# Doubling a block-triangular inverse: paired array corners and evictions on two engines

## The chip, the cores and the metric

The kernel runs on one core of a Trainium2 chip. The core has TensorE (PE in the views; PEld is its weight load), VectorE (DVE), ScalarE (ACT), GpSimd (POOL) and SyncE (SP), which run their own queues in order and wait for each other by semaphores. TensorE writes its results into PSUM, whose banks DVE or ACT then read out ("evict") to SBUF. The metric is the device time of one execution in microseconds, lower is better. Before the change it is 1331.12 us, the median of three runs (1328.65 to 1333.48).

## The reference, cut to what matters

One transformer block on 512 tokens with two mixers and an MLP. The part of interest is the gated delta rule in chunks: for each head and chunk a unit lower triangular matrix is inverted, and the inverse is used in the recurrence.

```python
k_beta = k * beta[..., None]
lower = jnp.where(strict, jnp.einsum('bhncd,bhnmd->bhncm', k_beta, k) * decay, 0.0)
eye = jnp.broadcast_to(jnp.eye(CHUNK, dtype=jnp.float32), lower.shape)
t_inv = lax.linalg.triangular_solve(lower, eye, left_side=True, lower=True, unit_diagonal=True)
u = jnp.einsum('bhncm,bhnme->bhnce', t_inv, v * beta[..., None])
w = jnp.einsum('bhncm,bhnmd->bhncd', t_inv, k_beta * jnp.exp(g_cum)[..., None])
```

The rest (projections, convolution, retention, gates, MLP) is large matrix products.

## The kernel before, in words

The delta rule runs on 8 heads and 4 chunks of 128 tokens, so there are 32 triangular matrices of 128x128, kept as `mt` (in the tile `acc`, fp32). `base_inverse` inverts their 32x32 diagonal blocks on DVE and leaves them in `rn` and, transposed, in `rt`; its last steps are two transposes on DVE (L1070, L1073), a copy on ACT (L1071) and eight copies on ACT of 32 partitions each into the diagonal of `rt` (L1077). `double_blocks` then doubles the inverted blocks twice, 32 to 64 and 64 to 128, by the formula for a block triangular inverse: the missing corner is minus inverse times corner times inverse, two products of small matrices. It works on two groups of 16 matrices (`m0` 0 and 16), in four products:

- the first (into `p1`) is corner times inverse, 32x32, for the two diagonal pairs of blocks (partitions 0 to 63 and 64 to 127), and its result goes by DVE into `y` (tile `mrb`, L1095);
- the second (`p2`) is inverse times that, again 32x32, into the corners of `rt` (L1107), and for the upper pair once more in transposed form into `rn` (L1109);
- the third (`p3`) and fourth (`p4`) are the same for the one pair of 64x64 blocks (L1118, L1127).

All these matmuls have both operands in fp32 and use a corner of the 128x128 array, whose rows follow from the partitions of the operands and whose columns from the partitions of the result. They are all issued from the helper at L668, in program order on TensorE (`keep_in_program_order`). Each product is done for group 0, then for group 1, each with a wait (`yield 1.5 * DB_US`) behind it. The PSUM banks are called `dl` and there are three of them in turn. All evictions are DVE's.

What stands between them is decided by a planner in Python, `Clock`. It keeps an estimate `now` of PE's time, to which each matmul adds its price (a 32x32 in fp32 0.059 us, a 64x64 0.113). Chains of dependent work yield the time after which they may go on, and until then the planner puts in pieces of the filler products (projections of `xs`, in three matmuls of 128x512 for each product of two split fp32 factors, `mm<-actT,whi` and `mm<-actT,wlo`). So each yield of 1.8 us puts nine filler matmuls between two small blocks. The same clock sets after which weight load a job of the sums is queued (`pace`: copies of weights on SP's queue, L169, and adds on POOL's, L135, one every 8.5 us of the planner's time). DVE's and ACT's orders are made by a scheduler from priorities, with `KEY_PRIO` for the evictions here. Other work there: the split of each weight load into two parts (ACT L148, DVE L149), and the convolution of the values (ACT L903, three times DVE L906, ACT L909).

Of the kernel before, what the change touches and what calls it, by code (L numbers as in the profile page):

```python
# [15 lines left out]
ALU = mybir.AluOpType  # L16
# [13 lines left out]
SMALL_US, CONV_US, TOK_US, PK_US, INV_US, DB_US = 10.5, 6.5, 2.5, 2.0, 46, 1.2  # L30
VT_US, KS_US, PX_US, PC_US, GATE_US, FEAT_US, INV_PRIO, CONV_PRIO, SMALL_PRIO, KEY_PRIO, DECAY_US, AHEAD, TR_US, REC_PRIO, OUT_PRIO, SUM_PRIO = 2.5, 2.4, 3.5, 2.4, 11.0, 1.0, 0, 600, 800, 600, 20.0, 700, 2.2, 900, 900, 300
# [32 lines left out]
def hybrid_block_kernel(ctx: ExitStack, tc: tile.TileContext, a: dict, out: bass.AP):  # L64
    nc = tc.nc
# [389 lines left out]
    rt = two_halves(pa, "rt", "f2", 16, P)  # L455
# [6 lines left out]
    with tc.tile_pool(name="xp", bufs=2) as xp:  # L462
# [3 lines left out]
        first = xp.tile([1, 1], F32, name="first", bufs=1)  # L466
# [101 lines left out]
        hi, lo = kept[0]  # L568
# [168 lines left out]
    clock = Clock()  # L737
# [190 lines left out]
    def acc_rows(t, half):  # L928
        return acc_t[:, t, half * 512 : half * 512 + 512]
# [54 lines left out]
    with delta_rule:  # L984
        mt = acc_tile = None
# [94 lines left out]
        def double_blocks():  # L1080
            groups = [(m0, slice(m0, m0 + 16), rn_all[0][:, m0 : m0 + 16, :]) for m0 in (0, 16)]
            ys = [rn_all[1][:, h, :].rearrange("p (n c) -> p n c", n=16) for h in (1, 0)]
            pairs = [(slice(b, b + 32), slice(b + 32, b + 64)) for b in (0, 64)]

            def bank(n):
                return psx.tile([P, T], F32, tag="dl", name="dl", bufs=3).rearrange("p (n c) -> p n c", n=n)

            for (m0, ns, rn), y in zip(groups, ys):
                p1 = bank(16)
                for lo, hi in pairs:  # L1090
                    for n in range(16):
                        clock.matmul(p1[hi, n, :], mt[lo, m0 + n, hi], rn[lo, n, 0:32], start=True, stop=True)
                with tc.high_priority(KEY_PRIO):
                    for lo, hi in pairs:
                        nc.vector.tensor_copy(y[hi, :, 0:32], p1[hi])  # L1095
                yield 1.5 * DB_US
            for (m0, ns, rn), y in zip(groups, ys):
                p2 = bank(16)
                for lo, hi in pairs:
                    for n in range(16):  # L1100
                        clock.matmul(p2[lo, n, :], y[hi, n, 0:32], rt[hi, m0 + n, hi], start=True, stop=True)
                hi = slice(32, 64)
                for n in range(16):
                    clock.matmul(p2[hi, n, :], rt[hi, m0 + n, hi], y[hi, n, 0:32], start=True, stop=True)
                with tc.high_priority(KEY_PRIO):
                    for lo, hi in pairs:
                        nc.vector.tensor_scalar(rt[lo, ns, hi], p2[lo], -1.0, None, ALU.mult)  # L1107
                    hi = slice(32, 64)
                    nc.vector.tensor_scalar(rn[hi, :, 0:32], p2[hi], -1.0, None, ALU.mult)  # L1109
                yield 1.5 * DB_US  # L1110
            lo, hi = slice(0, 64), slice(64, 128)
            for (m0, ns, rn), y in zip(groups, ys):
                p3 = [bank(8) for _ in range(2)]
                for n in range(16):
                    clock.matmul(p3[n // 8][hi, n % 8, :], mt[lo, m0 + n, hi], rn[lo, n, :], start=True, stop=True)
                with tc.high_priority(KEY_PRIO):
                    for i in range(2):
                        nc.vector.tensor_copy(y[hi, 8 * i : 8 * i + 8], p3[i][hi])  # L1118
                yield 1.5 * DB_US
            for (m0, ns, rn), y in zip(groups, ys):  # L1120
                p4 = [bank(8) for _ in range(2)]
                for n in range(16):
                    clock.matmul(p4[n // 8][lo, n % 8, :], y[hi, n, :], rt[hi, m0 + n, hi], start=True, stop=True)
                with tc.high_priority(KEY_PRIO):
                    for i in range(2):
                        js = slice(m0 + 8 * i, m0 + 8 * i + 8)
                        nc.vector.tensor_scalar(rt[lo, js, hi], p4[i][lo], -1.0, None, ALU.mult)  # L1127
                yield 1.5 * DB_US
            clock.done("doubled")

        vts, qfs, rqs, rows_of, ogs, zzs = {}, {}, {}, {}, {}, {}
# [302 lines left out]
        mt = acc.rearrange("p k t -> p (k t)").rearrange("p (n c) -> p n c", c=P)  # L1434
# [29 lines left out]
    with tc.tile_pool(name="pb", bufs=1) as pb_:  # L1464
# [129 lines left out]
        for h in range(4):  # L1594
# [398 lines left out]
```

## Time and profile before

| | before |
|---|---|
| median of 3 runs | 1331.12 us (1328.65 to 1333.48) |
| span of the profiled execution (the page gives no other time of it) | 1329.4 us |
| PE busy | 1314.3 us, 99% |
| DVE busy | 938.0 us, 71% |
| ACT busy | 663.9 us, 50% |
| mean granted TensorE clock | 0.997 |
| the doubling: first small matmul to the last one's block | 143.5 to 179.8 us |

The page's first part gives busy time, its share of the span and the number of instructions for each engine. In a timeline a row is a start, a duration (us), the engine, the line, the operation, result and operands by tile name, the form, and in brackets the idle time of the engine ahead of it with what ended that. An fp32 matmul leaves two records on PE. The ends of matmuls are modelled; their starts are not.

### The profile page before, as it was taken

How to read it: one execution, taken by the hardware profiler on the slowest of the kernel's cores; microseconds unless marked ns; L12 is line 12 of the kernel's file. 1: busy time of each engine (PE TensorE's matmuls, PEld its weight loads, DVE VectorE, ACT ScalarE, POOL GpSimd, SP SyncE). 2: the span in 40 equal slices, each digit the busy share in tenths (PEclk: the TensorE clock that was granted, in tenths of full speed). 3: DMA queues.
4: the chain of work that ended last, by engine and by line, in shares of the span. 5: the costliest groups of instructions: out<-in, count | busy, mean ns of one | idle time of the engine just before them, and what ended most of it. 6: DMA issues, size and time to landing. Idle time of an engine off the chain costs nothing.

```text
span 1329.4 us, 17531 instructions
## 1 busy us (share of the span) xinstructions
PE 1314.3 (99%) x6591; PEld 1093.6 (82%) x6591; DVE 938.0 (71%) x1569; ACT 663.9 (50%) x1159; POOL 89.6 (7%) x95
## 2 busy tenths in 40 slices
PE   9999999999999999999999999999999999999997
PEld 7888888888788888888888888888889888888886
DVE  6889867586656577877577766889675746738378
ACT  5784335555524533554453353455356636355364
POOL 2201100000010000000010000000001000000001
PEclk9999999999999999999999999999999999999999
DMA  6336944467765665986393472445629896868635
GB/s 191 133 112 159 203 101 94 110 164 194 188 159 151 143 187 142 270 244 155 95 259 89 104 229 80 141 150 173 233 78 248 225 275 147 234 187 225 188 118 135
DMA packets 115558, 223.16 MB, mean 168 GB/s; under 512 B 6983, under 2 KB 38897, under 8 KB 114961
## 3 DMA queue, kind: packets, MB, share of 16 engines
q1 hardware_dynamic: 96496, 175.13, 41.2%
q0 software_dynamic: 16944, 40.54, 18.9%
q10 hardware_dynamic: 2032, 6.36, 1.3%
q8 instruction: 52, 0.85, 0.2%
q14 instruction: 34, 0.27, 0.1%
HBM read 216.75 MB, written 72.37 MB: 217 GB/s over the span
## 4 chain that ended last, share of the span: by engine, by line
PE 89%; DVE 4%; ACT 4%; DMA 2%; issue 1%; DVEq 0%; ACTq 0%
PE mm L668 18%; PE mm L317 16%; PE dl L317 11%; PE mm L95 10%; PE mm L93 10%; PE mm L94 10%; PE dl L668 6%; DMA raw<-sums 1%; PE dl L93 1%; PE tr L397 1%; PE dl L95 1%; PE dl L94 1%; PE tr L677 1%; DVE wlo L149 1%; PE mm L632 1%
## 5 line engine op out<-in xcount | busy, mean ns | idle before, releaser
L149 DVE TENSOR_TENSOR wlo<-raw,whi 128x1024 fp32r<-128x1024 f32 x269 | 328.5, 1223 | 215.7 <-ACT whi L148 214.3
L148 ACT CAST whi<-raw 128x1024 fp32r<-128x1024 f32 x269 | 282.7, 1052 | 376.4 <-PE mm L668 74.6
L668 PE MATMUL mm<-actT,whi 128*128 128x512 f32 x448 | 144.8, 404 | 0.0
L317 PE MATMUL mm<-whi,xsum 128*128 128x512 f32 x384 | 120.6, 390 | 0.0
L95 PE MATMUL mm<-hn,wlo 128*128 128x512 f32 (+1 forms) x288 | 105.4, 366 | 0.0
L94 PE MATMUL mm<-hn,whi 128*128 128x512 f32 (+1 forms) x288 | 105.3, 366 | 0.0
L93 PE MATMUL mm<-hn,whi 128*128 128x512 f32 (+1 forms) x288 | 105.3, 366 | 0.0
L668 PEld LDWEIGHTS mm<-actT,whi 128*128 128x128 f32 x448 | 81.7, 190 | 15.3
L668 PE MATMUL mm<-actT,wlo 128*128 128x512 f32 x224 | 88.4, 395 | 0.0
L317 PEld LDWEIGHTS mm<-whi,xsum 128*128 128x128 f32 x384 | 71.8, 188 | 14.9
L317 PE MATMUL mm<-wlo,xsum 128*128 128x512 f32 x192 | 74.8, 390 | 0.0
L317 PE MATMUL dl<-whi,ffq 128*128 128x512 f32 x224 | 71.2, 389 | 0.0
L668 PE MATMUL mm<-whi,og 128*128 128x512 f32 x192 | 62.4, 397 | 0.0
L95 PEld LDWEIGHTS mm<-hn,wlo 128*128 128x128 f32 x288 | 54.3, 189 | 8.8
L94 PEld LDWEIGHTS mm<-hn,whi 128*128 128x128 f32 x288 | 54.3, 189 | 8.8
L93 PEld LDWEIGHTS mm<-hn,whi 128*128 128x128 f32 x288 | 54.3, 189 | 8.6
L668 PE MATMUL mm<-whi,actT 128*128 128x512 f32 x176 | 60.3, 405 | 1.0 <-DVE qf L906 1.0
L317 PE MATMUL dl<-whi,actT 128*128 128x512 f32 x192 | 61.2, 390 | 0.0
L317 PE MATMUL mm<-whi,ffq 128*128 128x512 f32 x192 | 60.9, 389 | 0.0
L1786 DVE TENSOR_TENSOR ffq<-r,ffq 128x512 fp32r<-128x512 f32 (+1 forms) x64 | 39.2, 622 | 27.8 <-ACT ffq L1786 27.6
L135 POOL DMA_DIRECT2D sums<-in_w_in_dram x28 | 32.6, 1164 | 364.3 <-DMA sums<-in_w_in_dram 364.3
L93 PE MATMUL mm<-actT,whi 128*128 128x512 f32 x128 | 51.5, 402 | 0.0
(391 smaller groups left out, 2843.0 us busy)
## 6 DMA issues: line engine op xcount, KB each, us to landing
raw<-in_w_in_dram SPq DMA_DIRECT2D x95, 512.0 KB, 4.6
raw<-sums SPq DMA_DIRECT2D x64, 512.0 KB, 4.5
raw<-in_w_up_dram SPq DMA_DIRECT2D x36, 512.0 KB, 7.1
sums<-in_w_in_dram SPq DMA_DIRECT2D x32, 512.0 KB, 5.6
sums<-in_w_down_dram SPq DMA_DIRECT2D x32, 512.0 KB, 7.4
sums<-in_w_in_dram POOLq DMA_DIRECT2D x28, 512.0 KB, 7.5
raw<-in_w_down_dram SPq DMA_DIRECT2D x24, 512.0 KB, 4.2
sums<-sums POOLq DMA_DIRECT2D x20, 512.0 KB, 8.4
```

The lines of the kernel that those rows point to most:

```text
L93: nc.tensor.matmul(ps, lh, rh, start=first, stop=False)
L94: nc.tensor.matmul(ps, lh, rl, start=False, stop=False)
L95: nc.tensor.matmul(ps, ll, rh, start=False, stop=last)
L135: tc.keep_in_program_order(nc.gpsimd.dma_start(dst, src, accum_op=ALU.add))
L148: nc.scalar.copy(hi[:, :n], raw[:, :n])
L149: nc.vector.tensor_tensor(lo[:, :n], raw[:, :n], hi[:, :n], ALU.subtract)
L317: m = nc.tensor.matmul(pss[t], lhs[i // 2], rhs[i % 2], start=first and k + i == 0, stop=k + i == 5, skip_group_check=not first,)
L397: nc.tensor.transpose(ps, src, ident)
L632: pin(nc.tensor.matmul(first_keys[f][:, 256:512], ws[w][:, kk, :], xs[x][:, 2 * j + kk, 256:512], start=False, stop=kk == 1 and i == 2, sk ...
L668: m = tc.keep_in_program_order(nc.tensor.matmul(*args, **kwargs))
L677: tc.keep_in_program_order(nc.tensor.transpose(ps, src, ident if by is None else by))
L1786: return nc.scalar.copy(dst[0], r), nc.vector.tensor_tensor(dst[1], r, dst[0], ALU.subtract)
```

## The change

`double_blocks` is written anew. The two groups go together: a helper `abreast` takes two or three lists of matmuls, issues one of each in turn, and counts their price in the planner's clock divided by the number of lists. In the first and second products group 0 works on one pair of blocks while group 1 works on the other, in two halves (`q`), so that neighbours have different rows and columns of the array. Each half is evicted right behind it, group 0 by DVE and group 1 by ACT. In the second product the transposed form (`right`) is a third list, for group 0 in the first half and group 1 in the second; DVE evicts it. The third and fourth products are cut into four units of 8 matrices: third products of units 0 and 1 alone, then third of unit 2 with fourth of unit 0, third of 3 with fourth of 1, then fourth of 2 and 3 alone. DVE evicts the third products, ACT the fourth. There are six places with filler in place of eight. What is computed is the same.

```diff
-            for (m0, ns, rn), y in zip(groups, ys):
-                p1 = bank(16)
-                for lo, hi in pairs:
-                    for n in range(16):
-                        clock.matmul(p1[hi, n, :], mt[lo, m0 + n, hi], rn[lo, n, 0:32], start=True, stop=True)
+            def abreast(*streams):
+
+                for step in zip(*streams):
+                    before = clock.now
+                    for args in step:
+                        clock.matmul(*args, start=True, stop=True)
+                    clock.now = before + (clock.now - before) / len(streams)
+
+            def first(g, q, p):
+                (m0, _, rn), (lo, hi) = groups[g], pairs[q]
+                return [(p[hi, n, :], mt[lo, m0 + n, hi], rn[lo, n, 0:32]) for n in range(16)]
+
+            def left(g, q, p):
+                (m0, _, _), (lo, hi) = groups[g], pairs[q]
+                return [(p[lo, n, :], ys[g][hi, n, 0:32], rt[hi, m0 + n, hi]) for n in range(16)]
+
+            def right(g, p):
+                m0, hi = groups[g][0], pairs[0][1]
+                return [(p[hi, n, :], rt[hi, m0 + n, hi], ys[g][hi, n, 0:32]) for n in range(16)]
+
+            p1 = [bank(16) for _ in range(2)]
+            for q in range(2):
+                abreast(first(0, q, p1[0]), first(1, 1 - q, p1[1]))
                 with tc.high_priority(KEY_PRIO):
-                    for lo, hi in pairs:
-                        nc.vector.tensor_copy(y[hi, :, 0:32], p1[hi])
+                    hi0, hi1 = pairs[q][1], pairs[1 - q][1]
+                    nc.vector.tensor_copy(ys[0][hi0, :, 0:32], p1[0][hi0])
+                    nc.scalar.copy(ys[1][hi1, :, 0:32], p1[1][hi1])
+            yield 1.5 * DB_US
+            p2 = [bank(16) for _ in range(2)]
+            for q in range(2):
+                abreast(left(0, q, p2[0]), left(1, 1 - q, p2[1]), right(q, p2[q]))
+                with tc.high_priority(KEY_PRIO):
+                    for g, (lo, hi) in ((0, pairs[q]), (1, pairs[1 - q])):
+                        dst = rt[lo, groups[g][1], hi]
+                        if g:
+                            nc.scalar.mul(dst, p2[g][lo], -1.0)
+                        else:
+                            nc.vector.tensor_scalar(dst, p2[g][lo], -1.0, None, ALU.mult)
+                    hi = pairs[0][1]
+                    nc.vector.tensor_scalar(groups[q][2][hi, :, 0:32], p2[q][hi], -1.0, None, ALU.mult)
+            yield 1.5 * DB_US
...
+            for u in range(2):
+                p = bank(8)
+                abreast(third(u, p))
+                keep_third(u, p)
+            yield 1.5 * DB_US
+            for u in range(2):
+                p3, p4 = bank(8), bank(8)
+                abreast(third(2 + u, p3), fourth(u, p4))
+                keep_third(2 + u, p3)
+                keep_fourth(u, p4)
                 yield 1.5 * DB_US
...
+            for u in range(2, 4):
+                p = bank(8)
+                abreast(fourth(u, p))
+                keep_fourth(u, p)
+            yield 1.5 * DB_US
             clock.done("doubled")
```

What this does to the order of instructions, first on PE, at the first product (`rn` and `acc` are its operands). Before:

```order
L668 MATMUL dl<-rn,acc 32x32 [waits DVE_49,PE_49]
L668 MATMUL dl<-rn,acc 32x32 x31
L668 MATMUL mm<-actT,whi 128x512 x2
L668 MATMUL mm<-actT,wlo 128x512
L668 MATMUL mm<-actT,whi 128x512 x2
L668 MATMUL mm<-actT,wlo 128x512
L668 MATMUL mm<-actT,whi 128x512 x2
L668 MATMUL mm<-actT,wlo 128x512
L668 MATMUL dl<-rn,acc 32x32 [waits PE_49]
L668 MATMUL dl<-rn,acc 32x32 x31
```

And after the change, at the same place:

```order
L668 MATMUL dl<-rn,acc 32x32 [waits DVE_49,PE_49]
L668 MATMUL dl<-rn,acc 32x32 [waits PE_49]
L668 MATMUL dl<-rn,acc 32x32 x30
L668 MATMUL dl<-rn,acc 32x32 [waits DVE_49]
L668 MATMUL dl<-rn,acc 32x32 [waits Activation_49]
L668 MATMUL dl<-rn,acc 32x32 x30
L668 MATMUL mm<-actT,whi 128x512 x2
L668 MATMUL mm<-actT,wlo 128x512
```

The two blocks of 32 now stand one behind the other, nine fillers have moved behind them, and the 33rd and 34th matmuls, the first of each list in the second half, have a wait for DVE and one for ACT.

ACT at the end of `base_inverse` (L1077) and the first product. Before:

```order
L1071 COPY rn<-rn 32x32x32 [waits DVE_49,Pool_49]
L1077 COPY rt<-mrb 32x16x32 [waits DVE_49]
L148 CAST whi<-raw 128x1024 [waits DMAHW1_49,PE_49]
L1077 COPY rt<-mrb 32x16x32 x5
L903 ACTIVATE vt<-mm,convw 128x512 [waits PE_49]
L1077 COPY rt<-mrb 32x16x32 x2
L148 CAST whi<-raw 128x1024 [waits DMAHW3_49,PE_49]
```

After the change; L1114 is the eviction of group 1's first product, L1123 that of its second:

```order
L1071 COPY rn<-rn 32x32x32 [waits DVE_49,Pool_49]
L1077 COPY rt<-mrb 32x16x32 [waits DVE_49]
L148 CAST whi<-raw 128x1024 [waits DMAHW1_49,PE_49]
L1077 COPY rt<-mrb 32x16x32 x4
L1114 COPY mrb<-dl 32x16x32 [waits PE_49,Activation_49]
L1077 COPY rt<-mrb 32x16x32 x2
L1114 COPY mrb<-dl 32x16x32 [waits PE_49]
L1077 COPY rt<-mrb 32x16x32
L903 ACTIVATE vt<-mm,convw 128x512 [waits PE_49]
L1123 ACTIVATE rt<-dl 32x16x32 [waits PE_49]
```

The first L1114 has come in behind the fifth L1077, the second behind the seventh, and L903 has moved behind all eight.

DVE after the change, from the last weight split ahead of the first product to the end of the second (L1113 evicts the first product of group 0, L1125 and L1127 the second, plain and transposed); before, its four L1095, four L1107 and two L1109 stood one by one between the same L906:

```order
L149 TENSOR_TENSOR wlo<-raw,whi 128x1024 [waits DMAHW1_49,PE_49,Activation_49]
L1113 COPY mrb<-dl 32x16x32 [waits PE_49] x2
L906 SCALAR_TENSOR_TENSOR vt<-mm,convw,vt 128x511 [waits DMASW0_49,Activation_49]
L906 SCALAR_TENSOR_TENSOR vt<-mm,convw,vt 128x510 [waits DVE_49]
L906 SCALAR_TENSOR_TENSOR vt<-mm,convw,vt 128x509 [waits DVE_49]
L1125 TENSOR_SCALAR rt<-dl 32x16x32 [waits PE_49]
L1127 TENSOR_SCALAR rn<-dl 32x16x32
L1125 TENSOR_SCALAR rt<-dl 32x16x32 [waits PE_49]
L1127 TENSOR_SCALAR rn<-dl 32x16x32 [waits Activation_49]
```

The ten evictions have become six, and the three L906 of one convolution stand ahead of the second product's. In the second product PE has, at the same place in the second half as above, a wait for DVE and one for ACT:

```order
L668 MATMUL dl<-rt,mrb 32x32 x2
L668 MATMUL dl<-mrb,rt 32x32
L668 MATMUL dl<-rt,mrb 32x32 [waits DVE_49]
L668 MATMUL dl<-rt,mrb 32x32 [waits Activation_49]
L668 MATMUL dl<-mrb,rt 32x32
```

Before, the 32 `dl<-rt,mrb` of a group stood first and its 16 `dl<-mrb,rt` behind them; now one `mrb,rt` follows each two `rt,mrb`.

More of the change, by code (lines that the diff above doesn't have):

```diff
@@ L1097, in double_blocks @@
[L1097 to L1128, printed above, removed]
+            def abreast(*streams):
[4 more added lines that the diff above has]
+                    clock.now = before + (clock.now - before) / len(streams)
```

19 lines of the change are left out of this document (added).

## The prediction

> **What bounds the kernel now.** The first part of the page, which gives the busy time of each engine, comes first, and after it the view of waits for TensorE alone (waiter, then what it waited for; us in total, times, longest).
>
> ```profile
> PE 1314.3 (99%) x6591; PEld 1093.6 (82%) x6591; DVE 938.0 (71%) x1569; ACT 663.9 (50%) x1159; POOL 89.6 (7%) x95
> ```
> ```profile
> PE tr L500 <- DMA nrow<-in_norm_mix_pre_dram: 0.8, 1, 0.8
> PE dl L668 <- DVE st L1320: 0.8, 1, 0.8
> PE dl L668 <- ACT vn L1311: 0.8, 1, 0.8
> ```
>
> TensorE (PE) is busy for 99% of the span and hardly waits: the longest waits are about 0.8 us. So a microsecond taken from PE's own work in the doubling is a microsecond of the kernel, and a microsecond for which PE has to stand still there is one too, for nothing later has slack to give it back. Next, the chain of work that ended last, cut to the stretch of the doubling (start us, us, what, instructions). The `dl` pieces with x64, x96 and x32 are the doubling; the `mm` pieces between them are filler products.
>
> ```profile
> 143.56 2.04 PE dl L668 x64
> 145.60 2.26 PE mm L668 x9
> 147.86 2.04 PE dl L668 x64
> 149.90 2.26 PE mm L668 x9
> 152.16 2.95 PE dl L668 x96
> 155.11 2.26 PE mm L668 x9
> 157.38 2.95 PE dl L668 x96
> 160.33 0.59 PE tr L677 x4
> 160.92 3.61 PE mm L668 x9
> 164.52 2.00 PE dl L668 x32
> ```
>
> The stretch is PE from end to end. Each fp32 matmul leaves two records, two passes: 64 records are the 32 matmuls of one group's first product. A 32x32 pass takes 2.04/64 = 31.9 ns, a 64x64 pass 2.00/32 = 62.5 ns. One piece stands out: nine filler matmuls take 2.26 us everywhere but at 160.92, where they take 3.61. The table of windows (window, its length, busy of PE, PEld, DVE, ACT, POOL, then PEclk, the granted TensorE clock, DMA share, GB/s) says why:
>
> ```profile
> 160.00:161.00 1.00, 1.00 (x17) 0.91 (x14) 0.64 (x2) 0.00 (x0) 0.00 (x0) 1.00 1.08 156
> 161.00:162.00 1.00, 1.00 (x4) 0.81 (x3) 0.97 (x3) 0.21 (x1) 0.00 (x0) 0.54 0.94 196
> 162.00:164.00 2.00, 2.00 (x6) 1.42 (x5) 1.79 (x3) 0.42 (x1) 0.00 (x0) 0.50 1.12 232
> 164.00:167.00 3.00, 3.00 (x36) 2.42 (x35) 1.13 (x2) 0.00 (x0) 0.00 (x0) 0.92 0.98 186
> ```
>
> The granted clock is 0.50 from 161 to a little past 164, right after 2.95 us of 32x32 matmuls, and 1.00 around it. One such fall costs 3.61 - 2.26 = 1.35 us here. The blocks of 2.04 us were not followed by one, nor was the first of 2.95.
>
> **The change part by part: what pairing saves.** Does PE run two corners of the array side by side? The timeline of PE where the second product goes from the corner of rows 96-127 (`dl<-rt,mrb`) to that of rows 32-63 (`dl<-mrb,rt`):
>
> ```profile
> 153.92 0.21 PE L668 MATMUL dl<-mrb,rt 32*32 32x32 f32 x1
> 153.95 0.19 PE L668 MATMUL dl<-rt,mrb 32*32 32x32 f32 x1
> 153.97 0.19 PE L668 MATMUL dl<-mrb,rt 32*32 32x32 f32 x1
> 153.98 0.19 PE L668 MATMUL dl<-rt,mrb 32*32 32x32 f32 x1
> 154.00 0.19 PE L668 MATMUL dl<-mrb,rt 32*32 32x32 f32 x1
> 154.01 0.19 PE L668 MATMUL dl<-rt,mrb 32*32 32x32 f32 x1
> 154.04 1.08 PE L668 MATMUL dl<-mrb,rt 32*32 32x32 f32 x29
> ```
>
> In program order all `rt,mrb` stand ahead of all `mrb,rt`, yet here they start in turn, and each corner keeps about its own 32 ns: seven starts in 0.12 us. So two corners with different rows do run at once, as far as PE looks ahead, and alternated code lets it do so throughout. I take the full factor of two for pairs with different rows. First product: 2 x 2.04 = 4.08 us become 2.04, **2.04 saved**. Second product: in each step two of the three matmuls have the rows 32-63, and nothing in the trace shows two corners of the same rows at once. One after the other, that strip has 2/3 of 192 passes, 128 x 31.9 ns = 4.08 us in place of 2 x 2.95 = 5.90, **1.82 saved**; if those paired too, 64 passes, 2.04 us, so the other end is 3.86 saved, and with no pairing 0. I take 1.82, by the strip that is seen to keep its period. Third and fourth product: four blocks of 32 passes, of which the last is
>
> ```profile
> 177.75 2.08 PE L668 MATMUL dl<-rt,mrb 64*64 64x64 f32 x32
> ```
>
> 4 x 2.00 = 8.00 us before. Now two of the four units of each product are paired with one of the other and four stand alone: 2 x 2.00 + 2 x 1.00 = 6.00, **2.00 saved** (0 to 2.00). Together 5.86 us.
>
> **The wait in the first product.** By the order, the 33rd and 34th small matmuls (the second half of the first product) now wait for DVE and ACT. They read the same tensors as the first 32, which wait for no ACT; what is new is that their banks have been handed to an eviction. So PE stands until both first evictions, L1113 on DVE and L1114 on ACT, are over, with the nine filler matmuls queued behind it. When can these run? ACT, then DVE, in the timeline:
>
> ```profile
> 144.40 0.62 ACT L1077 COPY rt<-mrb 32x512 f32<-32x512 f32 x1 [0.76 <-DVE rs_t L377]
> 145.04 1.04 ACT L148 CAST whi<-raw 128x1024 fp32r<-128x1024 f32 x1
> 146.11 2.93 ACT L1077 COPY rt<-mrb 32x512 f32<-32x512 f32 x5
> ```
> ```profile
> 146.12 1.23 DVE L149 TENSOR_TENSOR wlo<-raw,whi 128x1024 fp32r<-128x1024 f32 x1 [1.12 <-ACT whi L148]
> 147.38 1.41 DVE L1095 COPY mrb<-dl 32x512 f32<-32x512 f32 x2
> ```
>
> In the order after the change L1114 stands behind one L1077, the cast and four more L1077; nothing ahead of them has changed. Four of the five copies take 4/5 x 2.93 = 2.34 us and end at 148.45; an eviction of this size at 0.62 (I take the ACT copy of the same size from SBUF) ends at 149.07. DVE's first eviction is no help: 147.38 + 0.70 = 148.08. PE's first half, paired, ends at 143.56 + 1.02 = 144.58 and it goes on about 0.1 after the eviction, 149.17: a wait of **4.59 us**, which before was filled with the other half, nine fillers and the second group. What is saved by pairing the first half is thus only waited away again. Below, this could only be 0.11 + 0.62 + 0.1 = 0.83 us, if ACT were free.
>
> **The wait in the second product.** Here the second half waits for the second DVE eviction of the first half, L1127 behind L1125, in one bank. The nearest rows, PE's first matmul behind a small block and then DVE:
>
> ```profile
> 155.04 0.73 PE L668 MATMUL mm<-actT,whi 128*128 128x512 f32 x2
> ```
> ```profile
> 155.15 0.68 DVE L1107 TENSOR_SCALAR rt<-dl 32x512 f32<-32x512 f32 x1 [0.61 <-PE dl L668]
> 155.76 0.73 DVE L906 SCALAR_TENSOR_TENSOR vt<-mm,convw,vt 128x511 f32<-128x511 f32 x1
> 156.52 0.69 DVE L1107 TENSOR_SCALAR rt<-dl 32x512 f32<-32x512 f32 x1
> 157.22 0.68 DVE L1109 TENSOR_SCALAR rn<-dl 32x512 f32<-32x512 f32 x1
> ```
>
> DVE starts 0.11 us after PE is done, two evictions in a row take 157.90 - 156.52 = 1.38, and PE again some 0.1: **1.6 us**. At the least it is 0; at the most three L906 of 0.75 us, which stand ahead of L1125, are late and come on top, 3.85. I take 1.6: ACT's L903, which L906 needs, follows PE's first fillers at 151 and the first L1077 copies, and the three then end at about 154.5, when PE's first half ends (149.17 + 1.02 + 2.26 + 2.04).
>
> **The clock.** Before, 2.95 us of small matmuls brought one fall of 1.35 us. Now PE does 32x32 matmuls or nothing from 143.56 to 150.2, 6.6 us, and again for 2.04 + 1.6 + 2.04 = 5.7 us in the second product; I take one fall in each, two in place of one: **+1.35 us**. The ends are none (-1.35) and five in a row (+5.4), as each lasts some 3.4 us by the windows and the stretch about 20.
> The Trainium skill, "TensorE: Matmul & The Clock Gate", section "What's actually happening", says that the clock is halved by a free-running window of 3413 ns in which PE did too little. By that rule an idle stretch of 4.59 us lowers the clock even if small matmuls alone would not, and this trace agrees in the length of its one fall.
>
> **At no cost.** Eight of DVE's eighteen evictions go to ACT, 8 x 0.62 = 5.0 us. ACT has room for them once the L1077 copies are over; two of its rows there, with the idle time ahead in brackets:
>
> ```profile
> 161.79 0.63 ACT L909 ACTIVATE vt<-vt 128x512 f32<-128x512 f32 x1 [7.66 <-DVE vt L906]
> 168.37 1.05 ACT L148 CAST whi<-raw 128x1024 fp32r<-128x1024 f32 x1 [5.95 <-PE mm L668]
> ```
>
> The third and fourth products wait too, but for evictions that have nine fillers (2.26 us) or a whole block ahead of them, more than the 0.11 + 0.69 + 0.1 of one eviction; without that cover 0.9 us each. Since the planner's clock counts a paired step for less, it runs about 7.5 us behind its former course (by its own prices), and later steps of the recurrences and the jobs that copy and add sums slide by about one place past other loads on SP's and POOL's queues. PE waits for no such load in the view above, so I cost this at 0, with the two waits of 0.8 us either way: -1.6 to +1.6.
>
> **Sum.** -5.86 + 4.59 + 1.60 + 1.35 = **+1.7 us**. The profiled execution has a span of 1329.4 us and no other time of its own is shown; the median of the runs is 1331.12, 1.7 more, which I leave as it is for what lies around the span. 1331.1 + 1.7 = **1332.8 us**.
>
> **The rivals.** *The evictions come in time.* If the wait in the first product is 0.83 us and not 4.59, PE has no long hole, and with pairs that fill it twice as densely the clock need not fall at all: 3.76 + 2.70 less, 1326.3, faster. Against it stand the L1077 copies, which ACT does in order. *No pairing.* If alternating in code does not run corners at once beyond the few passes seen at a switch, 5.86 us are not saved, the first wait is 1.02 shorter, and one more fall of the clock comes: 1339.0, slower. It decides if passes still start 32 ns apart. The seven starts speak against it. *The clock stays down.* If the falls follow each other from the first wait through the second product, three more of 1.35: 1336.9, slower. For it speaks that the holes come 5 us apart; against it, that in the trace nine fillers ended a fall. *A floor under the start of a pass.* Passes of a pair could be held to a spacing above 16 ns; the seven starts have 0.12/6 = 20 on average. At that, the second half of the first product is 64 x 4 ns = 0.3 us longer, and the second product, 192 x 20 = 3.84, is not. 1333.1.
> The Trainium skill, same page, section "Wait — 56ns, not 53.3ns?", states a floor of about 25 ns from start to start. By it the estimate would be 64 x 9 ns and 192 x 25 ns - 4.08 us more, 1.3 us, 1334.1. The trace does not agree at its one such place: 20 ns.
>
> **How the numbers follow.** My forecast 0.57 (its own range 1328 to 1336), evictions in time 0.10, no pairing 0.13, the clock stays down 0.13, a floor 0.07. About 0.3%, 4 us, is what a measurement of this kernel can tell from no change: 1327.1 to 1335.1. Faster are the first rival and 0.03 of the forecast, 0.13; slower are no pairing, the low clock and 0.03 of the forecast, 0.29; within 0.58. The range, 1326.5 to 1339.0, runs from about the first rival, which is also the forecast with 2.04 of same-row pairing, 2.70 of clock and 1.6 of later waits off, to no pairing.
>
> **What would show it.** In the profile after: small passes with different rows start some 16 ns apart; the waits of PE gain one on ACT L1114 (or DVE L1113) of 4 to 5 us and one on DVE L1127 of about 1.6; the second product's halves take 2.0 us each, or 1.0 if same rows pair; the granted clock shows 0.5 in two stretches between 147 and 165 us. I am wrong if PE has no hole near 145, if the passes keep 32 ns, or if PE newly waits for a load after 200 us.

## The result, and the profile after

| | median us | runs | lowest to highest |
|---|---|---|---|
| before | 1331.98 | 6 | 1328.65 to 1333.80 |
| after | 1337.47 | 6 | 1336.08 to 1341.61 |

The ratio is 1.0056, with a 95% interval from 1.0039 to 1.0074: the change makes the kernel slower, by 0.6% by this ratio and by 5.5 us (0.4%) by the medians. Medians and ratios here leave out four executions in a slow state (1454 to 2705 us: one each of experiments 1, 3 and 7, one of the kernel before). The profiled execution of the kernel after took 1337.54 us with a span of 1335.8, 6.4 more than the 1329.4 of before. The readings below account for those 6.4 us.

The busy times of the engines, from the first part of the page after:

```profile
PE 1310.9 (98%) x6591; PEld 1089.5 (82%) x6591; DVE 930.7 (70%) x1561; ACT 668.0 (50%) x1167; POOL 90.4 (7%) x95
```

PE is busy for 3.4 us less than before and yet ends later, so it stood still for longer. The view of waits of the kernel after, PE alone (waiter, what it waited for; us in total, times, longest), says where:

```profile
PE dl L668 <- DVE mrb L1113: 3.4, 1, 3.4
PE dl L668 <- issue: 3.1, 1, 3.1
PE dl L668 <- DVE rn L1127: 2.4, 1, 2.4
...
PE dl L668 <- ACT mrb L1114: 0.7, 1, 0.7
```

All four are in the doubling, and none of them was there before. Two of them (L1113 with L1114, and L1127) stand in the prediction. The one on "issue", 3.1 us in which PE waits for nothing that the profile shows, does not. Next, the first product in the timeline of PE after:

```profile
143.68 1.20 PE L668 MATMUL dl<-rn,acc 32*32 32x32 f32 x64
148.29 0.31 PE L668 MATMUL dl<-rn,acc 32*32 32x32 f32 x2 [3.41 <-DVE mrb L1113]
149.34 1.91 PE L668 MATMUL dl<-rn,acc 32*32 32x32 f32 x62 [0.74 <-ACT mrb L1114]
```

The first half, 64 passes, takes 1.20 us where 64 took 2.04 (with the tail of its last pass; from start to start it is 1.03). Then PE stands until 149.34 but for two passes. ACT, in its timeline, shows why:

```profile
146.29 2.40 ACT L1077 COPY rt<-mrb 32x512 f32<-32x512 f32 x4
148.71 0.58 ACT L1114 COPY mrb<-dl 32x512 f32<-32x512 f32 x1
```

The eviction L1114 starts when the four copies end, and PE goes on at 149.34, 0.05 us behind it. But the second half, again 64 passes, takes 1.91 us and not 1.03. The rest is in the chain of work that ended last, from there to the fourth product (start us, us, what; pieces of some hundredths are left out):

```profile
149.34 1.91 PE dl L668 x62
151.26 2.87 PE mm L668 x6
...
154.15 0.70 ACT vt L903
...
154.88 0.76 DVE vt L906
...
157.19 0.59 DVE rt L1125
...
157.79 0.69 DVE rn L1127
...
158.53 1.80 PE dl L668 x86
160.33 3.12 issue
163.45 0.42 PE dl L668 x6
163.87 4.14 PE mm L668 x9
...
170.02 2.27 PE mm L668 x9
172.29 1.08 PE dl L668 x32
```

Three things are to be seen. Six fillers take 2.87 us at 151.26 and nine take 4.14 at 163.87, where nine took 2.26 before and take 2.27 again at 170.02: PE is at about half its rate. The second wait, up to 158.53, is a chain: the sixth filler, then L903 on ACT at 154.15, three L906, L1125, L1127. And six passes before the end of the second product PE stops for 3.12 us. The table of windows after (window, its length, busy of PE, PEld, DVE, ACT, POOL, PEclk, DMA share, GB/s):

```profile
144.00:147.50 3.50, 0.89 (x56) 0.77 (x50) 2.26 (x6) 2.86 (x5) 0.85 (x1) 1.00 1.05 329
147.50:151.00 3.50, 1.97 (x63) 1.83 (x64) 0.70 (x2) 2.97 (x6) 0.00 (x0) 0.50 0.91 92
151.00:154.30 3.30, 3.30 (x15) 2.60 (x12) 0.70 (x1) 1.34 (x3) 0.68 (x2) 0.50 0.95 236
154.30:157.70 3.40, 1.81 (x99) 1.29 (x97) 2.75 (x4) 1.54 (x3) 2.35 (x3) 0.99 1.01 219
157.70:160.00 2.30, 1.47 (x83) 1.47 (x86) 0.76 (x2) 0.21 (x1) 0.10 (x1) 0.51 1.01 128
160.00:163.50 3.50, 0.38 (x21) 0.25 (x15) 0.00 (x0) 0.00 (x0) 0.00 (x0) 0.50 1.06 168
163.50:168.00 4.50, 4.50 (x20) 3.11 (x20) 1.37 (x2) 0.97 (x2) 0.00 (x0) 0.50 0.45 83
```

The clock is at 0.50 from 147.5 to 154.3 and again from 157.7 to 168, 17 us in all, where before there were about 3.4. In the stretch ahead of each fall PE was busy for 0.89 us of 3.5 and 1.81 of 3.4; behind 4.50 of 4.5 the clock is back. In the window 160.00:163.50 PE, DVE, ACT and POOL all do next to nothing, so no engine's work can be what PE waits for there; only the DMA engines are full, with a share of 1.06.

One row of the same table, asked for the first half of the second product, shows what pairing does:

```profile
154.90:155.95 1.05, 1.05 (x97) 1.05 (x96) 1.01 (x2) 0.00 (x0) 0.71 (x1) 1.00 1.10 228
```

96 passes in 1.05 us, 10.9 ns from start to start, at full clock: all three corners of a step run at once, also the two that have the same rows.

**The account.** Pairing: the first product takes 2 x 1.03 in place of 4.08, the second 2 x 1.03, from first start to last, in place of 5.90 (both at full clock), and two paired blocks of 1.08 (172.29 is one) stand where 2 x 2.00 stood: -2.02 - 3.84 - 1.84 = **-7.7 us**. The first wait: 149.34 - (143.68 + 1.03) = **+4.6**. The second: **+2.4**. The hole: **+3.1**. The low clock: second half of the first product 1.91 - 1.03 = 0.9, the fillers behind it (154.90 - 151.26) - 2.26 = 1.4, second half of the second product 1.80 + 0.42 - 1.03 = 1.2, fillers 4.14 - 2.26 = 1.9, less the 1.35 that the fall of before cost: **+4.0**. The sum is +6.4, the difference of the spans. It is good to some tenths: the second wait is 2.4 in the view of waits and would be 2.6 from start to start, as the first one is counted.

### The profile page after: what moved, and what is told of

Read it like the earlier page. It is cut to its first block, busy times and chain, and to the rows that moved or that the text cites. A ratio compares the mean times of both kernels' runs of the same rounds, so it can differ in the third digit from the quotient of the medians.

```text
span 1335.8 us, 17525 instructions
## 1 busy us (share of the span) xinstructions
PE 1310.9 (98%) x6591; PEld 1089.5 (82%) x6591; DVE 930.7 (70%) x1561; ACT 668.0 (50%) x1167; POOL 90.4 (7%) x95
## 4 chain that ended last, share of the span: by engine, by line
PE 86%; DVE 6%; ACT 4%; DMA 2%; issue 1%; DVEq 0%; ACTq 0%
PE mm L668 17%; PE mm L317 17%; PE dl L317 11%; PE mm L93 10%; PE mm L94 10%; PE mm L95 10%; PE dl L668 6%; PE tr L397 1%; DVE wlo L149 1%; PE dl L94 1%; PE dl L95 1%; PE dl L93 1%; PE tr L677 1%; DMA raw<-sums 1%; PE mm L632 1%
```

## The experiments

The runs of the kernel before lay between medians of 1330.0 and 1332.2 us from one set of runs to the next, so ratios to the kernel before of the same set are compared. The kernel after has 1.0056 (1.0039 to 1.0074).

**1. Evictions behind both halves** (of the kernel after):

```diff
             for q in range(2):
                 abreast(first(0, q, p1[0]), first(1, 1 - q, p1[1]))
+            for q in range(2):
                 with tc.high_priority(KEY_PRIO):
...
                 abreast(left(0, q, p2[0]), left(1, 1 - q, p2[1]), right(q, p2[q]))
+            for q in range(2):
                 with tc.high_priority(KEY_PRIO):
```

> The kernel after, but the evictions of the first and of the second product are issued behind both of their halves, so TensorE does not stand still between the halves. Theory (the two waits in the middle, 4.65 and 2.4 us, and the falls of the clock that follow them, make up the loss): both waits go; a wait of at most 2 us may come ahead of the second product, where ACT is still behind its five copies; some 8 us come back, about 1329.5 us. Rival (TensorE uses up its instructions faster than the DMA queues bring new ones, as in the hole of 3.1 us near 160 us): the hole comes earlier, inside the second product at about 151.6 us, and is as long or up to 4 us; about 1330.5 to 1334 us. Rival (the time was lost in later steps that the planner moved): no more than 1 us comes back, 1336.5 us or more.

Median 1329.65 us, ratio 0.9986 (0.9975 to 0.9997): 0.7% back, and slightly below the kernel before. The chain in the second product of this kernel:

```profile
150.42 2.14 PE dl L668 x180
152.56 4.55 issue
157.11 0.42 PE dl L668 x10
157.54 4.14 PE mm L668 x9
```

Both waits in the middle are gone, and one of 0.8 us on ACT's L1115 stands ahead of the product. So the waits made up most of the loss. The falls of the clock did not go with them, against my theory: the clock is at 0.50 for 17.1 us at a stretch (153.2 to 170.3), as long as in the kernel after in all, and nine fillers again take 4.14 us. The hole stays too, and is longer: 4.55 us. It comes ten passes before the end of the second product, close to where it came after the change (six), though the product now begins 4.5 us earlier and has no wait in it. The hole follows the place in the program, not the time. The profiled execution, with a span of 1331.1 us, began 1.3 us late (last section) and is one of the slower of this kernel.

**2. Pairing in place** (of the kernel before; groups, fillers and evictions as they were):

```diff
-                for lo, hi in pairs:
-                    for n in range(16):
+                for n in range(16):
+                    for lo, hi in pairs:
                         clock.matmul(p1[hi, n, :], ...)
...
-                for lo, hi in pairs:
-                    for n in range(16):
+                for n in range(16):
+                    for lo, hi in pairs:
                         clock.matmul(p2[lo, n, :], ...)
-                hi = slice(32, 64)
-                for n in range(16):
+                    hi = slice(32, 64)
                     clock.matmul(p2[hi, n, :], ...)
```

> The kernel before, with one thing of the change: within each half of the columns the small matmuls of different array corners alternate in the first and second product; the order of the halves, the filler products between them, the evictions on VectorE and the third and fourth product stay as before. Theory (pairing pays by itself, same rows too, and the loss of the change came from putting the halves together): 2.0 + 3.8 us less than before, about 1326 us, with no wait between the products over 0.5 us. Rival (the refill of instructions bounds the stretch): a hole of 1 to 3 us shows in it, 1327 to 1329 us. Rival (shorter bursts of small matmuls let the clock fall more often): two or three falls of 1.35 us, 1329 to 1331 us.

Median 1327.21 us, ratio 0.9965 (0.9953 to 0.9977), the lowest ratio of all, though not clear of experiments 9 and 12: 4.6 us less than before in the same set. The chain of this kernel, second product:

```profile
150.43 1.14 PE dl L668 x96
...
153.83 0.84 PE dl L668 x67
154.67 2.62 issue
157.29 0.51 PE dl L668 x29
```

96 passes take 1.14 us in place of 2.95, with no wait for an eviction anywhere: VectorE's evictions run beside the fillers. What is left over is the hole, here after 67 of the second group's 96 passes, as the first rival said. The doubling accounts for only part of the gain: the block after the last `dl` piece begins at 177.34 us and not at 179.82, 2.5 us earlier, while the span is 4.0 us shorter (1325.4). The rest came later, where TensorE waits less (14.0 us of idle time beside the hole in the whole span, against 15.1), and was not traced.

**3. The streams in turn** (of the kernel after, without alternation):

```diff
-                for step in zip(*streams):
-                    before = clock.now
-                    for args in step:
+                before = clock.now
+                for stream in streams:
+                    for args in stream:
                         clock.matmul(*args, start=True, stop=True)
-                    clock.now = before + (clock.now - before) / len(streams)
+                clock.now = before + (clock.now - before) / len(streams)
```

> The kernel after, with the streams of small matmuls issued one after the other and not alternating; waits, evictions and the planner's clock stay. Theory (pairing is worth 7.7 us on TensorE and only waits, clock and the hole ate it): passes go back to some 32 ns; the first half's extra 1.0 us is waited away, the hole of 3.1 us goes since instructions are used up at half the pace: +7.7 - 1.0 - 3.1 = +3.6 us, about 1341 us. Rival (pairing is worth little): within 1 us of the kernel after, 1337.5 us.

Median 1341.67 us, ratio 1.0070 (1.0056 to 1.0084): 1.9 us more than the kernel after by the ratios, whose intervals overlap, 4.2 by the medians and 5.3 by the spans of the profiled executions (1341.1 and 1335.8). The profile shows the parts: the hole is gone, and the blocks are longer and at half clock:

```profile
148.12 3.43 PE dl L668 x64
...
155.69 4.90 PE dl L668 x96
```

So with the halves together, pairing brings less than the 7.7 us that it takes off PE, for part is waited away or goes into the hole. How much is left, from next to nothing by the ratios to some 5 us by the spans, this run does not settle.

**4. The program shifted by 108 instructions** (of the kernel after). The 18 warm-up matmuls at the start, each a weight load and a matmul, become 72 of a quarter of the columns, which adds 54 x 2 = 108 TensorE instructions and changes nothing in the doubling:

```diff
-                tc.keep_in_program_order(nc.tensor.matmul(pw, warm[:, 0:P], warm, start=True, stop=True))
+                for i in range(4):
+                    c = slice(P * i, P * i + P)
+                    tc.keep_in_program_order(nc.tensor.matmul(pw[:, c], warm[:, 0:P], warm[:, c], start=True, stop=True))
```

The reason: in the trace two DMA queues carry only instructions, q8 and q14, and the count of q8 fits TensorE. In the kernel after, its row of the whole run (packets, MB, share of 16 engines) and of the window 160 to 163 us:

```profile
q8 instruction: 52, 0.85, 0.3%
```
```profile
q8 instruction: 1, 0.02, 4.8%
```

52 packets of 0.85 MB / 52 = 16 KB for 2 x 6591 = 13182 TensorE instructions (matmuls and loads): one per about 254, which fits blocks of 256. One packet is in the window of the hole, at work for 4.8% x 16 x 3 us = 2.3 us; from 147.9 to 160.1 us there is none.

> The kernel after, with each of the 18 warm-up matmuls at the very start split into four of a quarter of the columns: 108 more TensorE instructions, the same columns. Everything else stands at the same places, but each block of 256 instructions ends 108 instructions earlier in the program. Theory (the hole of 3.1 us near 160 us is TensorE out of instructions, waiting for a late refill): the refill is now asked for some 4 us earlier, between the first and the second product, the hole goes or falls under 0.5 us, about 1334.4 us. Rival (the hole belongs to this place in the doubling, whatever the refills do): it stays after about 90 passes of the second half, 1337.5 us.

Median 1333.34 us, ratio 1.0010 (1.0002 to 1.0019). The hole is gone:

```profile
158.50 1.93 PE dl L670 x66
160.42 4.11 PE mm L670 x9
```

Adding instructions at the start made the kernel faster than the kernel after by 0.46% (the intervals are apart), and the two other waits stay at 3.4 and 2.5 us. A hole that belonged to this place would have stayed.

**5. The copying jobs rest during the doubling** (of the kernel after; TensorE's order is the same):

```diff
-        queued[0] += JOB_US
+        queued[0] = 175.0 if 125.0 < queued[0] + JOB_US < 175.0 else queued[0] + JOB_US
```

> The kernel after, with the jobs that copy and add sums resting while the planner's clock is between 125 and 175 us, so that their DMA traffic is not there during the doubling; TensorE's instructions and their order are the same. Theory (the refill comes late because the DMA engines are full, mostly with these jobs): the refill near 155 us starts within about 1 us of being due, the hole of 3.1 us goes, about 1334.4 us if the jobs that come later cost nothing. Rival (the refill is late for another reason): the hole stays within 1 us of its length, 1337.5 us.

Median 1334.58 us, ratio 1.0032 (1.0019 to 1.0045). The time is the one expected by the theory (by the ratios 3.2 us less than the kernel after, though the intervals overlap), but the hole does not go altogether:

```profile
160.31 0.89 issue
161.20 0.43 PE dl L668 x8
```

It begins at the same place, as the same instructions are used up, and ends 2.2 us earlier. So the refill is late because of the traffic of these jobs in good part; what makes up the other part (the weight loads are left) was not tried.

**6 to 8. The shift again, on other kernels.** All three have the split warm-up of experiment 4. The sixth is the pairing in place with the third and fourth product of the change as well, the seventh the pairing in place alone, the eighth the kernel before.

> All that has paid so far in one kernel: the halves in turn with corners alternating within each (as in the pairing in place), the third and fourth product as in the change (two of the four units of the one paired with the other, evictions of the fourth on ScalarE), and 108 more TensorE instructions at the start by splitting the warm-up. Theory: from 1327.2 us the hole (2.6), the fall of the clock behind it (1.4) and the pairing of the third and fourth product (1.84) come off, about 1321.4 us. Rival (other refills come due at a worse place, or the paired units wait for banks): a new hole of 1 to 3 us, 1322.5 to 1324.5 us. Faster than both kernels by either.

> The pairing in place, with the warm-up split as before (108 more TensorE instructions at the start). Theory (the hole of 2.6 us near 154.7 us is a late refill, and the low clock after 158.3 us follows from the hole): the hole goes and the nine fillers that took 3.64 us take 2.26 again: 1327.2 - 2.6 - 1.4 = 1323.2 us. Rival (the clock falls there because of the small matmuls, as in the kernel before): the fall stays, 1324.6 us. Rival (the hole is not a refill): 1327.2 us.

> Control: the kernel before with the warm-up split in the same way (108 more TensorE instructions). The kernel before has no hole in the doubling, so by the theory of the refill nothing is to be gained: 1331.8 us, within 0.7. Rival (the split warm-up itself saves 2 to 4 us, which would explain the 1333.3 us without any refill): 1328 to 1330 us.

The control came out as expected, 1.0007 (0.9994 to 1.0020). The other two did not gain what they should: 0.9997 (0.9987 to 1.0007) for the sixth, medians 1330.20 against 1330.02, and 0.9989 (0.9977 to 1.0001) for the seventh, no better than the 0.9965 without the shift. In the chain of the seventh the hole did not go. It moved:

```profile
155.48 0.27 PE dl L670 x13
155.75 1.40 issue
157.15 1.08 PE dl L670 x83
158.22 0.59 PE tr L679 x4
158.81 2.08 PE mm L670 x9
160.89 2.00 PE dl L670 x32
162.89 2.48 issue
```

Without the shift it came after 67 passes of the block (experiment 2), now after 13: 54 passes earlier, which are 108 instructions, exactly those added at the start. And between the first hole and a second one, of 2.48 us, lie 83 + 4 + 9 + 32 = 128 matmuls with their loads, 256 instructions. In the sixth the hole stands at the same place, after 13 passes, with 1.98 us, and a wait of 2.3 us for ScalarE (`vt`, L1361) has come up later. My expectation was wrong in that a shift would hide the hole: in the pairing in place it came with both borders that were tried. That the hole is TensorE out of instructions is shown by it all the better. Counted in the traces, TensorE's queue (matmuls, weight loads and a few others) has started the same 2241 instructions before the hole in every kernel that has one, with the shift (experiments 6 and 7) and without, and 2497, which is 256 more, before the second hole of the seventh. And each time PE goes on 1.0 to 1.6 us after a packet of q8 has ended.

**9. Fillers between the halves** (of the kernel after):

```diff
                     nc.scalar.copy(ys[1][hi1, :, 0:32], p1[1][hi1])
+                if q == 0:
+                    yield 1.5 * DB_US
...
                     nc.vector.tensor_scalar(groups[q][2][hi, :, 0:32], p2[q][hi], -1.0, None, ALU.mult)
+                if q == 0:
+                    yield 1.5 * DB_US
```

> The kernel after, with nine filler products put between the two halves of the first and of the second product as well (the planner's clock moves on for them as at the other places); pairing and evictions stay. Theory (TensorE standing still between the halves costs twice, by the wait and by the clock that falls after it): the first wait shrinks from 4.8 to about 2.4 us, the second goes, no clock fall follows the first product, and with a hole of 0 to 2 us some 9 us come back: 1327.5 to 1329.5 us. Rival (the clock falls because of the small matmuls, not because of the standing still): the falls stay, 1331 to 1333 us. Rival (the second wait comes from VectorE's queue, whatever the clock): it stays at 2.4 us, 1330 to 1332 us.

Median 1326.88 us, ratio 0.9977 (0.9964 to 0.9989): 0.8% less than the kernel after, from nine fillers at two places. Its windows:

```profile
144.00:148.00 4.00, 3.03 (x58) 2.26 (x51) 2.72 (x7) 3.44 (x6) 0.85 (x1) 1.00 0.87 276
148.00:152.00 4.00, 2.99 (x68) 2.56 (x69) 2.13 (x4) 3.85 (x7) 0.00 (x0) 0.81 0.93 109
152.00:156.00 4.00, 4.00 (x105) 3.08 (x105) 1.78 (x3) 2.10 (x4) 1.72 (x2) 0.76 0.87 277
```

The clock is low for one stretch inside 148 to 156 us, in place of 17 us, behind a wait of 1.2 + 0.8 us that is left in the first product. The wait for L1127 (here L1129) is 0.7 us, and there is no hole: the fillers leave the refill its time.

**10 and 11. About 18 fillers behind each group**, with pairing in place; the eleventh has the third and fourth product of the change too:

```diff
-                yield 1.5 * DB_US
+                yield 3.0 * DB_US
```

> The pairing in place, with about twice the filler products behind each group of the first and second product (18 or so in place of nine), so that 256 instructions take longer to use up. Theory (the hole appears where 292 instructions last less than the refill takes, some 4 to 5 us late and 1 us long): no hole over 0.5 us, and no fall of the clock behind it, 2.6 + 1.4 us less than the pairing in place, about 1323.2 us. Rival (later work of the recurrences now starts 9 us later and TensorE waits for it): 1325 to 1328 us. Rival (no change): 1327.2 us.

> As the pairing in place with twice the filler products, and the third and fourth product as in the change. Theory: two blocks of 2.0 us become 1.08 each, 1.84 us less than without: about 1321.4 us. Rival (the later wait for an eviction of ScalarE that came up with this pairing, 2.3 us, stays): 1323 to 1324.5 us. Rival (the smaller the blocks, the more often the refill is late): a new hole of 1 to 2.5 us, 1323 to 1325 us.

The tenth has 1330.64 us, 0.9996 (0.9983 to 1.0008), the eleventh 1327.63 us, 0.9983 (0.9968 to 0.9997). Both were expected lower, at 1323.2 and 1321.4. In the eleventh a hole of 0.30 us is left (160.58), and its profiled span is 1323.1. In the profiled execution of the tenth the doubling is as expected, without hole or fall, and yet its span is 1325.5, the 1325.4 of the pairing in place: waits of about 1 us each show later, for instance 1.1 us for ACT at L923, which the pairing in place does not have. Its runs spread from 1325.25 to 1332.16, those of the pairing in place from 1325.62 to 1328.32. By its rival the later start of the recurrences takes the gain; that is in line with those waits, but where the slower of the runs lose their time was not seen.

**12. About 18 fillers between the halves of the first product**, the rest as in experiment 9:

> As the kernel with nine fillers between the halves, but with about 18 of them between the halves of the first product. Theory (the rest of the first wait, 1.2 + 0.8 us, is uncovered time behind ScalarE's copies, and the one fall of the clock left near 150.5 us comes from it): both go, 2.0 + 1.4 us less than 1326.9 us, about 1323.5 us in the profiled execution, and the granted clock stays 1.00 from 144 to 185 us. Rival (the fall comes from the small matmuls, not from the standing still): the fall stays, 1325 us. Rival (other waits later take the gain, as in the kernels with twice the fillers): 1326 to 1328 us with no wait and no fall in the doubling.

Median 1327.55 us, ratio 0.9974 (0.9959 to 0.9989), the same as experiment 9 within the intervals. The doubling is as the theory has it but for one wait in the second product. Windows of this kernel:

```profile
148.00:152.00 4.00, 3.99 (x76) 3.14 (x75) 2.11 (x4) 3.92 (x7) 0.00 (x0) 1.00 1.02 115
...
156.00:160.00 4.00, 2.58 (x93) 1.94 (x93) 2.95 (x5) 0.75 (x2) 2.17 (x2) 1.00 0.94 199
```

The first wait is gone, and the clock stays at 1.00. But the second wait is 1.4 us here, with the three L906 again ahead of it, at full clock. And this execution was late before the doubling began, as the last section tells. So the gain in the first product is shown by the profile, not by the time.

## Why the prediction was wrong, step by step

The forecast was 1332.8 us, no change to be measured, with 0.29 for slower; it became slower by 5.5. The range, up to 1339.0, held the time. Two steps failed above all: instructions that arrive late had no term (+3.1 us in the kernel after), and the low clock was put at +1.35 us and measured +4.0. Step by step:

- **"PE from end to end".** Right: the busy time of PE fell by 3.4 us, its idle time rose from 15.1 to 24.9, and the sum is the 6.4 of the spans. (The longest waits of PE before were 1.2 and 1.0 us, for L464 and L906, and not about 0.8; neither lies in the doubling.)
- **Pairing, 5.86 us saved.** Right as a mechanism, too small in size: 7.7. The term that failed is the second product's 1.82, taken "by the strip that is seen to keep its period". Corners with the same rows run at once too (96 passes in 1.05 us); the other end that the text gives, 3.86, is what came, 3.84.
- **The wait in the first product, 4.59 us.** Right: 4.6, with L1114 behind four L1077 copies as worked out. Experiments 9 and 12 confirm it by filling it.
- **The wait in the second product, 1.6 us.** Too small: 2.4, inside its bounds of 0 and 3.85. The step that failed is that the three L906 are over "when PE's first half ends". L903 waited for the sixth of the nine fillers, the L906 ran from 154.88 to 157.19, and PE's first half, paired, took 1.03 us and not 2.04, so that it ended some 1.1 us before them. With 2.04 the wait would have been about 1.4 (an estimate: 2.4 less the 1.0); so about half of what pairing saved beyond the forecast in the second product was waited away. The half rate of the fillers is not the reason: the last three, behind which the first half starts, took 0.77 us, as at full clock.
- **The clock, +1.35 us.** Wrong in size, and the largest of the mis-sized terms: +4.0. "One fall in each" assumed that nine fillers end a fall. They did, but only at the end of a stretch of their own; each fall lasted two or three stretches of 3.4 us (147.5 to 154.3 and 157.7 to 168), in the first of which PE again did little (1.97 us of 3.5; 1.47 of 2.3, then 0.38 of 3.5 in the hole). The rival "the clock stays down" had this, at 1336.9, the nearest of the times given; but that it came so near is luck, for it has 5.4 us of clock where 4.0 were measured, 1.9 too little pairing and no hole. The standing still is a cause: in experiments 9 and 12 the same paired matmuls run, and with it filled there is one fall, then none. It is not the only one: in the kernel before the clock fell with PE busy throughout, right after 2.95 us of unpaired small matmuls, and in experiment 1 it stayed down from 157.1 to 170.3 us, where PE worked without a pause on fillers and 64x64 blocks. The Trainium skill, "TensorE: Matmul & The Clock Gate", section "What's actually happening", has a window of 3413 ns; 6.8 and 10.2 us are two and three of those.
- **No term for a hole of 3.1 us.** This is the step that is missing altogether. The text costed instructions by PE's time alone and never asked whether they arrive. Experiments 4, 5 and 7 and the count of 2241 instructions show the cause: paired, 96 passes with their loads use 192 instructions in about 1 us, the next block of 256 is late by some microseconds while the DMA engines are full, and PE runs dry. Before, 192 instructions took 2.95 us, with fillers between. The Trainium skill, "Runtime: NRT & Kernel Launch", section "Instruction fetch mechanics", speaks of blocks of 256 instructions, fetched by a DMA queue of the sequencer's own, and calls the cost of a crossing mostly hidden. The size agrees with the trace (128 matmuls with loads from hole to hole); hidden it is not, with holes of 0.3 to 4.55 us.
- **"At no cost".** The planner's shift and the later waits were put at 0. Right within some tenths: of PE's 24.9 us of idle time 9.7 are the waits and the hole in the doubling, which leaves 15.2 against 15.1 before.

The other errors, -1.9 for pairing, +0.8 for the second wait and +2.6 for the clock, make +1.6 us together: 1334.4 without the hole, against the 1333.3 of experiment 4, where it is gone. What the change could have brought is shown by experiments 2, 9 and 12: 0.2 to 0.35% faster than before, once nothing makes PE stand between two halves.

## What to carry to other kernels

Alternate small matmuls of different corners inside a block whose order stays as it is, and hand a bank to an eviction only when other work of PE stands between it and the next write to that bank; look also at what is queued ahead of that eviction on its engine. Price an idle stretch of PE with the clock that follows it: here 4.6 + 2.4 us of waits and a hole of 3.1 brought another 4.0. Where PE gets through 256 instructions in less than a few microseconds under heavy DMA traffic, count the refills of instructions as a resource of the stretch, and keep wide matmuls among the small ones.

## What the runs showed of the hardware that had not been expected

- **Three corners at once, two of them with the same rows.** 96 passes of 32x32 in 1.05 us, 10.9 ns from start to start. The Trainium skill, "TensorE: Matmul & The Clock Gate", section "Wait — 56ns, not 53.3ns?", has a floor of about 25 ns for a start; across corners this case lies below it.
- **TensorE out of instructions.** Holes of 0.3 to 4.55 us in seven kernels of this study, each of an engine that waits for nothing else. They come after the same 2241 instructions in all seven, so they move by 54 passes when 108 instructions are put in at the start, and two of them lie 256 instructions apart.
- **The clock's rise at the start varies with the execution.** In the twelfth kernel the ten warm-up matmuls (timeline of PE, second row: the kernel after) took 4.09 us, in others 2.33:

```profile
5.75 4.09 PE L475 MATMUL warm<-warm 128*128 128x512 bf16 x10
```
```profile
5.45 2.33 PE L475 MATMUL warm<-warm 128*128 128x512 bf16 x10
```

In the traces the first record of the full clock begins 9.35 us into this execution and 4.15 into the other (the table of windows gives 1.00 even ahead of the first record). That execution came to its first wide products (L550) at 11.82 us and not at 10.68, 1.1 us late, with the same instructions. The profiled executions of the first, seventh and eighth experiment began 1.1 to 1.5 us late too, with a first record at 9.4 to 10.3 us. One execution's span can differ from another's by that much before any change is looked at.
